# A two-layer diffusion step: the last gate blocks by token group, output weights loaded among them, projection tiles in the order of the attention, scratch tensors with long runs

## The chip, the cores and the metric

One core of a Trainium2 chip runs the whole step. The metric is the device time of one execution in microseconds (us). The engines are named as in the profile: PE (TensorE matmul), PEld (its weight load), DVE (VectorE), ACT (ScalarE), POOL (GpSimd), and SP (SyncE), which issues all the DMAs that this text speaks of from one queue, in order.

## The reference, cut to what matters

Layer 0 projects 1280 tokens (1024 latent, 256 context) into two attentions with a SiLU gate each; the gated outputs meet in one output projection. Layer 1 is a Fourier mixer with its own gate and projection.

```python
def even_lat(h, w_in, w_out, gq, gk, sink, ka_ctx, va_ctx, kb_ctx, vb_ctx, cos, sin):
    qa, ka, va, ga, qb, kb, vb, gb = even_projections(h, w_in, gq, gk)
    ...
    oa = dense_block_attention(qa, jnp.concatenate([ka, ka_ctx], axis=1),
                               jnp.concatenate([va, va_ctx], axis=1))
    ob = window_attention_with_ctx(qb, kb, vb, kb_ctx, vb_ctx, sink)
    return jnp.concatenate([oa * jax.nn.silu(ga), ob * jax.nn.silu(gb)], axis=-1) @ w_out

def odd_mix(h, w_in, w_out):
    u, gate = jnp.split(h @ w_in, 2, axis=-1)
    return (fourier_mix(u) * jax.nn.silu(gate)) @ w_out
```

## The kernel before, in words

All matmuls are float32 products made of split operands: a tensor `x` is held as `hi` and `lo`, and `mm3` adds three products. So every weight and every activation costs a copy on ACT (`hi`) and a subtraction on DVE or POOL (`lo`) before PE can use it.

The ten token tiles of 128 are worked through in units (tile, group, pair). A unit is `soft` (scores, exponentials) and, some units later, `weigh` (transposes `pt`, products `av`, a store into the DRAM scratch `od`). The tiles of mixer A come first, then those of mixer B in the order `ORD_B`. When a tile's last unit is done, `totals` sends its softmax sums through a transpose (`tt`) into the scratch `scd`.

Between units `attend` pumps a filler queue: each unit gives a credit of a few us (`FILL_B`, `FILL_C`), and queued pieces of other work are written into the program as far as the credit reaches. In order, the queue holds the remaining projections, the gate blocks `gate0` (three token groups `gi` of 512, 512 and 256 tokens, for each of eight column tiles; psum `ga`, result into scratch `gd`), the folded Fourier weights `fold_piece` (psum `wa`, result into scratch `wcd` and `wsd`), and the output projection of layer 0 by row tile. In the kernel before, the eight output weights `w_out0` are loaded and split by `out_weights` among the last eight fold pieces, into the buffers that the normalised activations (`hbufs`) held until the last gate block.

The output projection has ten steps. `proj_load` reads one row tile `r` back from `od`, `gd` and `scd` (`proj_in`), multiplies the three (`pm`), splits the product, and `proj_step` runs 48 matmuls (psum `oz`, two halves of 512 columns: `oz20` and `oz21` are the halves of row tile 2). The order of row tiles is `PAIRS`. A row tile needs certain attention tiles (`USES`: the tokens are permuted, so row tile 5 needs attention tiles 6 and 7), and `can_run` lets a load into the program only when those tiles have been finished for more than two units; from the third pair on (`EARLY`) only after the attention. In the attention the `pm` products are on POOL, after it on DVE.

A scheduler with a timeline of its own then fixes each engine's order; each engine runs its own list in order and waits by semaphores. Later, `u_load` reads the folded weights back for the Fourier mixer.

Of the kernel before, what the change touches and what calls it, by code (L numbers as in the profile page):

```python
# [28 lines left out]
ORD_B = (0, 2, 3, 4, 7, 5, 1, 6, 8, 9)  # L29
# [9 lines left out]
)  # L39
USES = ((0,), (1,), (2, 3), (2, 3), (4, 7), (6, 7), (4, 6), (5,), (8,), (9,))  # L40
# [86 lines left out]
def hybrid_step(ctx: ExitStack, tc: tile.TileContext, I, O):  # L127
# [278 lines left out]
    hbufs = []  # L406
# [27 lines left out]
    def h_slot(gi, k):  # L434
        n = GROUPS[gi][1]
        kper, slots = hT[gi]
        if k % kper == 0:
            hh = take("u", (P, kper, n * P), F32R)
            hl = take("u", (P, kper, n * P), F32R)
            slots.append((hh.a, hl.a))  # L440
            hbufs.extend([hh, hl])
        return [x[:, k % kper, :] for x in slots[k // kper]]
# [92 lines left out]
    def fold_piece(g, kb2, wu, tag="g", later=None):  # L535
# [11 lines left out]
        def put():  # L547
            rows = slice(kb2 * 256, kb2 * 256 + 256)
            sp.dma_start(wcd[g // 2, rows, g % 2, :].rearrange("(k p) f -> p k f", p=P), wo[:, :, 0:129])
            sp.dma_start(wsd[g // 2, rows, g % 2, :].rearrange("(k p) f -> p k f", p=P), wo[:, :, 128:256])  # L550
            drop(wo)
# [224 lines left out]
    def gate0(ct, gi, w):  # L776
# [10 lines left out]
        if gi < 2:  # L787
# [9 lines left out]
            sp.dma_start(gd[ct, :, t0 * P : t0 * P + 512], gs.a)  # L797
        else:
            silu(gs[:, 0:P], th[:, 0:P], acc[:, 0:P])
            silu(gs[:, P : 2 * P][:, ::-1], th[:, P : 2 * P], acc[:, P : 2 * P])  # L800
            sp.dma_start(gd[ct, :, 1024:1152], gs[:, 0:128])
            sp.dma_start(gd[ct, :, 1153:1280], gs[:, 128:255])
            sp.dma_start(gd[ct, :, 1152:1153], gs[:, 255:256])
# [174 lines left out]
    def totals(t):  # L978
# [5 lines left out]
        dve.reciprocal(tot, tot)  # L984
        tp = t_bank(f"tt{t}")
        pe.transpose(tp[0:16, 0:P], tot, ident)
        row = take("e", (16, P))
        store(scd, row, t, lambda out: act.activation(out, tp[0:16, 0:P], AF.Copy))  # L988
        drop(row)

    def store(dst, buf, t, fill):
        rev = t in (2, 3, 6, 7, 9)
        fill(buf[..., ::-1] if rev else buf.a)
        for c0, b0, n in PLACE[t]:
            sp.dma_start(dst[..., c0 : c0 + n], buf[..., b0 : b0 + n])

    def weigh(t, g, pr, bufs, p, tiles):
# [25 lines left out]
        dst = od[2 * g + pr].rearrange("(h d) n -> d h n", d=64)  # L1023
# [4 lines left out]
        def put():  # L1028
            for c0, b0, n in PLACE[t]:
                sp.dma_start(dst[..., c0 : c0 + n], os_[..., b0 : b0 + n])  # L1030
            drop(os_)
# [63 lines left out]
    for i, nm in enumerate(order):  # L1095
# [14 lines left out]
        else:  # L1110
            for c in range(2):
                for gi in range(3):
                    work.append((5.3 if gi < 2 else 2.7, lambda ct=2 * j + c, gi=gi, nm=nm: gate0(ct, gi, ws[nm])))
        nxt = loader(order[i + 1]) if 0 < i < len(order) - 1 else None
        if nxt is not None:
            fl_.add(0.0, nxt)
        after_g3 = order.index("g3") < i
        if i == order.index("g3") + 1:
            fl_.add(0.0, lambda: drop(*hbufs) or 0)
            wk_left = deque(range(8))  # L1120
            every = max(1, 4 * (len(order) - i) // 8)
            count = 0
        for n, w in enumerate(work):
            fl_.add(*w)
            if after_g3:
                count += 1
                if count % every == 0 and wk_left:
                    fl_.add(0.0, lambda k=wk_left.popleft(): wout.extend(out_weights(I["w_out0"], (k,), UV)) or 0)
        if nm[0] != "f":
            fl_.add(0.0, releaser(nm))  # L1130

# [40 lines left out]
    def proj_in(src, gate, r, resid):  # L1172
        cols = slice(r * P, r * P + P)
        if gate is not None:
            flush_held()
            ol = take(OB[0], (P, 8, P))
            sp.dma_start(ol.a, src[:, :, cols].rearrange("c p t -> p c t"))
            gl = take(OB[0], (P, 8, P))
            rl = take(OB[0], (P, 8, P))
            sp.dma_start(gl.a, gate[:, :, cols].rearrange("c p t -> p c t"))  # L1180
            sv = scd.rearrange("(c h) n -> h c n", h=2)
            for h in range(2):
                sp.dma_start(rl[64 * h : 64 * h + 64], sv[h, :, cols].unsqueeze(0).to_broadcast([64, 8, P]))
# [86 lines left out]
    half = []  # L1270
# [12 lines left out]
    def proj_step(i, j):  # L1283
# [17 lines left out]
        if r == 4:  # L1301
# [25 lines left out]
        half.append((xe, xo_))  # L1327
        if i % 2 == 0:
            return 0
        (eh, oh), (el, ol) = half  # L1330
        half.clear()
# [6 lines left out]
        if 0 in pairs[i]:  # L1338
            act.activation(op[0:1, :], oh[0:1, :], AF.Copy)
        pick("fq", E_FQ).tensor_sub(oh.a, ol.a, oh.a)  # L1340
        if 0 in pairs[i]:
            act.activation(oh[0:1, :], ol[0:1, :], AF.Copy)
        drop(ol)
        quads[pairs[i][0]] = (ep, eh, op, oh)
# [33 lines left out]
    while pend:  # L1378
        u0, pt0 = pend.pop(0)
        weigh(*u0, *pt0)  # L1380
        after(u0)
# [86 lines left out]
    def cos_src(hf):  # L1468
        return wcd[hf].rearrange("k g f -> k (g f)")

    def sin_gap(hf):
        def fn(raw, r0):
            v = raw.a.rearrange("p j (g f) -> p j g f", g=2)
            for g in range(2):
                sp.dma_start(v[:, :, g, :], wsd[hf, r0 : r0 + 2 * P, g, :].rearrange("(j p) f -> p j f", p=P))
            pool.memset(v[:, :, :, 0:1], 0.0)
        return fn

    def u_load(n):
# [14 lines left out]
        if c == 0:  # L1494
            return load_w(cos_src(hf), width=258, tags=("u", "w", "p"), each=row)
        return load_w(None, tags=BIG, gap=sin_gap(hf))
# [413 lines left out]
```

## Time and profile before

| | us |
|---|---|
| median of 3 runs | 1223.39 |
| lowest, highest | 1222.12, 1226.59 |
| profiled execution, device time | 1225.89 |
| its span, first to last instruction | 1224.1 |
| PE busy in the span | 1164.8 |
| DVE busy in the span | 841.6 |

The span is 1.8 us shorter than the device time of the same execution, and that execution is 2.5 us above the median. PE is the engine to look at: an idle microsecond of PE is a microsecond of the kernel, and one of another engine is not. The stretches that the change touches are, in the profile of before, the gate blocks (607 to 700), the folds with the output weights (700 to 747), the first three steps of the output projection beside the last attention units (747 to 795), the end of the attention (795 to 812) and the remaining steps of the projection (to about 900).

### The profile page before, as it was taken

How to read it: one execution, taken by the hardware profiler on the slowest of the kernel's cores; microseconds unless marked ns; L12 is line 12 of the kernel's file. 1: busy time of each engine (PE TensorE's matmuls, PEld its weight loads, DVE VectorE, ACT ScalarE, POOL GpSimd, SP SyncE). 2: the span in 40 equal slices, each digit the busy share in tenths (PEclk: the TensorE clock that was granted, in tenths of full speed). 3: DMA queues.
4: the chain of work that ended last, by engine and by line, in shares of the span. 5: the costliest groups of instructions: out<-in, count | busy, mean ns of one | idle time of the engine just before them, and what ended most of it. 6: DMA issues, size and time to landing. Idle time of an engine off the chain costs nothing. (4 is left out here: it accounts for less than half of the span.)

```text
span 1224.1 us, 21997 instructions
## 1 busy us (share of the span) xinstructions
PE 1164.8 (95%) x8103; PEld 1038.7 (85%) x8103; DVE 841.6 (69%) x1990; ACT 580.1 (47%) x1163; POOL 314.9 (26%) x274
## 2 busy tenths in 40 slices
PE   7879999999999999999999988989999999999997
PEld 5768889999999998999999877767877888997886
DVE  4387888877676776678878777667765963368543
ACT  4342466555565565556666676422365224332211
POOL 2254643513221231010000123120412225444001
PEclk9999999999999999999999999979999999999999
DMA  9957312323414242344233497777203435354321
GB/s 335 340 177 273 87 59 74 93 85 105 142 62 127 66 134 75 106 117 129 67 119 107 128 274 200 189 218 199 104 27 130 155 121 148 122 178 161 128 96 60
DMA packets 148688, 168.82 MB, mean 138 GB/s; under 512 B 19754, under 2 KB 107606, under 8 KB 148580
## 3 DMA queue, kind: packets, MB, share of 16 engines
q1 hardware_dynamic: 148580, 167.41, 44.1%
q8 instruction: 64, 1.05, 0.4%
q14 instruction: 44, 0.36, 0.1%
HBM read 123.19 MB, written 44.18 MB: 137 GB/s over the span
## 5 line engine op out<-in xcount | busy, mean ns | idle before, releaser
L1010 DVE TENSOR_TENSOR pt<-pt,pt 128x512 fp32r<-128x512 f32 (+1 forms) x264 | 171.3, 658 | 41.4 <-ACT pt L263 40.8
L263 ACT ACTIVATE pt<-pt 128x512 fp32r<-128x512 f32 (+1 forms) x265 | 147.4, 577 | 99.9 <-PE pt L1007 59.4
L1013 PE MATMUL av<-pt,u 128*128 128x256 f32 x1008 | 170.4, 290 | 2.2 <-DVE e L1025 1.5
L1007 PE MATMUL pt<-identr,p 128*128 128x128 f32 x1008 | 155.0, 272 | 3.0 <-ACT e L988 1.6
L1013 PEld LDWEIGHTS av<-pt,u 128*128 128x128 f32 x1008 | 140.7, 190 | 7.4 <-DVE e L1025 2.3
L251 PE MATMUL q<-w,u 128*128 128x256 f32 x864 | 133.0, 289 | 1.9 <-DVE u L427 1.6
L1007 PEld LDWEIGHTS pt<-identr,p 128*128 128x128 f32 x1008 | 118.7, 140 | 9.7 <-DVE pt L1010 2.1
L251 PE MATMUL ga<-u,w 128*128 128x512 f32 (+1 forms) x576 | 124.5, 359 | 0.0
L251 PEld LDWEIGHTS q<-w,u 128*128 128x128 f32 x864 | 116.2, 190 | 6.8 <-DVE u L427 1.9
L931 ACT ACTIVATE p<-p,nm 128x1280 f32<-128x1280 f32 (+1 forms) x80 | 95.3, 1192 | 56.1 <-DVE p L924 52.7
L251 PEld LDWEIGHTS ga<-u,w 128*128 128x128 f32 x576 | 93.8, 188 | 13.4
L269 POOL TENSOR_TENSOR w<-h,w 128x512 fp32r<-128x512 f32 x42 | 56.5, 1363 | 124.6 <-DVE w L265 87.6
L890 PE MATMUL sL<-u,q 128*128 128x512 f32 x256 | 82.2, 412 | 3.8 <-DMA q<-qd 3.7
L931 ACT ACTIVATE p<-p,NM 128x640 f32<-128x640 f32 (+2 forms) x80 | 59.1, 740 | 24.5 <-DVE p L924 24.3
L251 PE MATMUL oz<-u,u 128*128 128x512 f32 x240 | 64.3, 403 | 3.3 <-DVE h L1206 2.0
L890 PE MATMUL sC<-u,q 128*128 128x256 f32 x320 | 63.9, 299 | 1.9 <-DMA q<-qd 1.9
L269 POOL TENSOR_TENSOR u<-h,u 128x512 fp32r<-128x512 f32 x18 | 24.2, 1346 | 154.3 <-ACT u L263 139.3
L924 DVE TENSOR_SCALAR_CACHE_REDUCE p<-sL 128x512 f32<-128x512 f32 x64 | 43.8, 685 | 25.6 <-PE pt L1007 12.8
L251 PEld LDWEIGHTS oz<-u,u 128*128 128x128 f32 x240 | 45.6, 193 | 14.5 <-issue 2.4
L666 POOL TENSOR_TENSOR h<-h,rope 128x512 f32<-128x512 f32 (+1 forms) x18 | 21.6, 1203 | 139.3 <-ACT h L749 100.2
L251 PE MATMUL kv<-w,u 128*128 128x256 f32 x384 | 55.8, 288 | 0.0
L890 PEld LDWEIGHTS sC<-u,q 128*128 128x128 f32 x320 | 49.4, 190 | 5.5 <-issue 2.3
(790 smaller groups left out, 2608.4 us busy)
## 6 DMA issues: line engine op xcount, KB each, us to landing
q<-qd SPq DMA_DIRECT2D x80, 256.0 KB
p<-i_ada_w SPq DMA_DIRECT2D x21, 512.0 KB
h<-i_w_in SPq DMA_DIRECT2D x40, 256.0 KB
h<-i_w_out SPq DMA_DIRECT2D x32, 256.0 KB
pt<-i_ada_w SPq DMA_DIRECT2D x14, 512.0 KB
qd<-q SPq DMA_DIRECT2D x22, 256.0 KB
u<-g1d SPq DMA_DIRECT2D x9, 512.0 KB
w<-i_wuT SPq DMA_DIRECT2D x8, 512.0 KB
```

What stands on the lines that cost most here:

```text
L251: pe.matmul(out, a, b, start=i == 0, stop=i == n - 1)
L263: act.activation(out, in_, AF.Copy)
L269: pick("lo" + lc, lc).tensor_sub(dst_l, src, dst_h)
L666: pick("rope", XE["rope"]).tensor_mul(t1.rearrange("p t h (b c) -> p t (h b) c", b=2), y.rearrange("p t h (b c) -> p t (h b) c", b=2), cb)
L890: pe.matmul(ps, q_at(q, s, hc), keys, start=s == 0, stop=s == 1)
L924: dve.tensor_scalar(p[i][:, end[i] : end[i] + n], ps, sign, last[i], op0=ALU.mult, op1=ALU.min, accum_out=c)
L931: act.activation(p[i][:, 0 : end[i]], p[i][:, 0 : end[i]], AF.Exp, bias=last[i], scale=-1.0, accum_out=SU[:, t, hd + i, 0:1],)
L1007: pe.transpose(tp[:, jj * 256 + i * P : jj * 256 + i * P + P], p[i][:, off : off + P], ident)
L1010: dve.tensor_sub(pt[:, 1, 0:n], tp[:, 0:n], pt[:, 0, 0:n])
L1013: pe.matmul(acc, vv, pt[:, s, jj * 256 : jj * 256 + 256], start=c + jj + s == 0, stop=c + jj == nt - 1 and s == 1,)
```

## The change

Three things are done. **First**, the gate blocks of the last two weight blocks (`g2`, `g3`: four column tiles) run by token group: all four for group 0, then all four for group 1, then for group 2. After each group its `hbufs` are given back, and the output weights take their place: four weights among the blocks of group 1, four among those of group 2. The folds `f2` and `f3` follow with no output weights among them. `f2` and `f3` are also loaded only after both gate weight blocks are released. **Second**, `ORD_B` and `PAIRS` are changed: row tiles 0, 4, 2, 6 are projected first, and attention tile 6 comes sixth and no longer eighth. **Third**, `od`, `gd` and `scd` are laid out by row tile, so that a load reads runs of 4 KB where it read 512 bytes, and `wcd` and `wsd` become one `wd` with one store per fold piece. Beside this, an attention tile whose place crosses a row tile by one token is stored in two pieces (`PIECES`), a gate block of 512 tokens is stored in four runs of 512 bytes and no longer one of 2 KB, and the cosine half of the Fourier weights is read in two DMAs of 516-byte runs and no longer one of 1032.

```diff
-ORD_B = (0, 2, 3, 4, 7, 5, 1, 6, 8, 9)
+WSTEP = ((2, 1, 2), (1, 0, 1))
+ORD_B = (0, 2, 3, 4, 7, 6, 5, 1, 8, 9)
...
+PIECES = tuple(
+    tuple((r, max(c0, r * P) - r * P, b0 + max(c0, r * P) - c0, min(c0 + n, r * P + P) - max(c0, r * P))
+          for c0, b0, n in runs for r in range(c0 // P, (c0 + n - 1) // P + 1))
+    for runs in PLACE
+)
...
-PAIRS = ((3, 7), (1, 5), (2, 6), (0, 4), (8, 9))
+PAIRS = ((0, 4), (2, 6), (3, 7), (1, 5), (8, 9))
...
-ORDER = "qa0 qa1 kb0 qb0 qb1 f1 g0 g1 g2 g3 f0 f2 f3"
+ORDER = "qa0 qa1 kb0 qb0 qb1 f1 f0 g0 g1 g2 g3"
+FLATE = "f2 f3"
...
-    od = dr.tile([8, P, NT * P], F32, name="od")
-    gd = dr.tile([8, P, NT * P], F32, name="gd")
-    wcd = dr.tile([2, D, 2, 129], F32, name="wcd")
-    wsd = dr.tile([2, D, 2, P], F32, name="wsd")
+    od = dr.tile([NT, P, 8, P], F32, name="od")
+    gd = dr.tile([NT, P, 8, P], F32, name="gd")
+    wd = dr.tile([2, D, 2, 256], F32, name="wd")
...
-    scd = dr.tile([16, NT * P], F32, name="scd")
+    scd = dr.tile([NT, 2, 8, P], F32, name="scd")
...
-            sp.dma_start(gd[ct, :, t0 * P : t0 * P + 512], gs.a)
+            sp.dma_start(gd[t0 : t0 + 4, :, ct, :].rearrange("r p n -> p r n"), gs.a.rearrange("p (r n) -> p r n", r=4))
...
-            for c0, b0, n in PLACE[t]:
-                sp.dma_start(dst[..., c0 : c0 + n], os_[..., b0 : b0 + n])
+            for r, c0, b0, n in PIECES[t]:
+                dst = od[r, :, 2 * g + pr, c0 : c0 + n].rearrange("(h d) n -> d h n", d=64)
+                sp.dma_start(dst, os_[..., b0 : b0 + n])
...
+    for gi in range(3):
+        for n, (jj, c) in enumerate([(int(nm[-1]), c) for nm in order[-2:] for c in range(2)]):
+            fl_.add(*gate_work(jj, c, gi))
+            if gi > 0 and n % WSTEP[gi - 1][0] == WSTEP[gi - 1][1]:
+                wout_next(WSTEP[gi - 1][2])
+        fl_.add(0.0, lambda gi=gi: drop(*hbufs[gi]) or 0)
+    for nm in order[-2:]:
+        fl_.add(0.0, releaser(nm))
+    wout_next(len(wk_left))
+    for nm in FLATE.split():
+        fl_.add(0.0, loader(nm))
+        for k in range(4):
+            fl_.add(FC, lambda k=k, nm=nm: fold_piece(int(nm[1]), k, ws[nm]))
...
-            sp.dma_start(ol.a, src[:, :, cols].rearrange("c p t -> p c t"))
+            sp.dma_start(ol.a, src[r])
...
-                sp.dma_start(rl[64 * h : 64 * h + 64], sv[h, :, cols].unsqueeze(0).to_broadcast([64, 8, P]))
+                sp.dma_start(rl[64 * h : 64 * h + 64], scd[r, h].partition_broadcast(64))
...
-                sp.dma_start(v[:, :, g, :], wsd[hf, r0 : r0 + 2 * P, g, :].rearrange("(j p) f -> p j f", p=P))
-            pool.memset(v[:, :, :, 0:1], 0.0)
+                sp.dma_start(v[:, :, g, :], wd[hf, r0 : r0 + 2 * P, g, cols].rearrange("(j p) f -> p j f", p=P))
+            if c == 1:
+                pool.memset(v[:, :, :, 0:1], 0.0)
```

`totals` also reorders its 16 sums by a small DVE copy `byp`, ten times in all.

Line numbers of the changed program are five to fourteen above those of before for the same statement. Three places show how the order moves.

**ACT, from the first fold piece of `f2` on.** `h..<-wa20` evicts a fold piece, `u..<-h..` is the `hi` copy of an output weight that a DMA brought into `h..`, `e..<-tt7` copies the sums of tile 7. Before:

```order
L263 ACTIVATE h887_9111<-wa20_9106 128x512
L263 ACTIVATE pt915_9268<-pt7_312_9263 128x512
L1022 ACTIVATE e901_9185<-av7_30_9160 64x256
L263 ACTIVATE pt931_9360<-pt8_200_9355 128x512
L931 ACTIVATE p913_9229,SU_106<-p913_9229,NM_107 128x640
L263 ACTIVATE u920_9299<-h922_9301 128x512
L988 ACTIVATE e918_9287<-tt7_9285 16x128
L263 ACTIVATE h892_9130<-wa21_9125 128x512
L263 ACTIVATE pt952_9445<-pt8_210_9440 128x512
L263 ACTIVATE u904_9198<-h906_9200 128x512
```

Now:

```order
L269 ACTIVATE h917_9207<-wa20_9202 128x512
L936 ACTIVATE p929_9285,SU_105<-p929_9285,NM_106 128x640
L269 ACTIVATE pt931_9325<-pt7_312_9320 128x512
L1027 ACTIVATE e923_9259<-av7_30_9234 64x256
L936 ACTIVATE p929_9285,SU_105<-p929_9285,NM_106 128x640
L269 ACTIVATE pt939_9399<-pt8_200_9394 128x512
L997 ACTIVATE e934_9346<-tt7_9344 16x128
L269 ACTIVATE h918_9215<-wa21_9210 128x512
L936 ACTIVATE p937_9368,SU_105<-p937_9368,NM_106 128x640
L269 ACTIVATE pt952_9462<-pt8_210_9457 128x512
```

The two copies of output weights are gone from between the evictions; all sixteen stand earlier, among the gate blocks.

**SP, around the store of the first finished projection step (`x1d`).** `u1041` from `od` is the load of step 3 (row tile 5) before; `w1005`, `u1006` and `u1007` are the loads of step 3 (row tile 6) now. Before, with the last query load at the top:

```order
L895 DMA q1002_9875<-qd_69 64x2x512 x2
...
L1306 DMA x1d_76<-w990_9742 128x1024
L1183 DMA q1043_10188<-scd_78 64x8x128 x2
L1183 DMA u1065_10366<-scd_78 64x8x128 x2
L1195 DMA w1077_10452<-i_xp 128x1024
L1030 DMA od_72<-e1013_9963 64x2x128
L1177 DMA q1072_10439<-od_72 128x8x128
L1177 DMA u1041_10185<-od_72 128x8x128
L1195 DMA w1055_10272<-i_xp 128x1024
```

Now:

```order
L1196 DMA u1007_9926<-scd_77 64x1024 x2
...
L1191 DMA w1005_9923<-od_72 128x1024
L900 DMA q1019_10012<-qd_69 64x2x512 x2
L1194 DMA u1006_9925<-gd_73 128x1024
L1035 DMA od_72<-e992_9772 64x2x127
L1035 DMA od_72<-e992_9772 64x2x1
L1208 DMA w983_9690<-i_xp 128x1024
L1319 DMA x1d_75<-w950_9442 128x1024
```

The reads of `od` and `scd` for step 3 stood behind the second `x1d` store; they stand now, with that of `gd`, ahead of the first, around the last query load.

**PE, at the end of the attention.** `av9_31` is the last product of the last attention tile; `oz51` is step 3 before, `oz61` is step 3 now. Before:

```order
L251 MATMUL oz20_10380<-u888_9115,w1053_10268 128x512
L251 MATMUL oz20_10380<-u889_9116,w1053_10268 128x512
L1013 MATMUL av8_31_10106<-pt1030_10112,u685_7043 128x256 x4
L986 MATMUL tt9_10174<-identr_86,tot9_10168 16x128
L251 MATMUL oz51_10302<-u888_9115,q1044_10194 128x512
L251 MATMUL oz51_10302<-u889_9116,q1044_10194 128x512
L251 MATMUL oz21_10408<-u888_9115,w1053_10268 128x512
L251 MATMUL oz21_10408<-u889_9116,w1053_10268 128x512
L1013 MATMUL av9_30_10134<-pt1034_10140,u685_7043 128x256 x4
L251 MATMUL oz51_10302<-u888_9115,p1045_10195 128x512
L251 MATMUL oz51_10302<-u893_9134,q1044_10194 128x512
```

Now, first where step 3 begins, then behind the last attention product:

```order
L1012 MATMUL pt1_314_10150<-identr_85,p998_9860 128x128 x2
L257 MATMUL oz61_10332<-u817_8407,u1008_9932 128x512
L257 MATMUL oz61_10332<-u818_8408,u1008_9932 128x512
...
L1018 MATMUL av9_31_10256<-pt1046_10262,u685_7046 128x256 x4
L257 MATMUL oz70_10486<-u817_8407,pt1066_10404 128x512
L257 MATMUL oz70_10486<-u818_8408,pt1066_10404 128x512
L257 MATMUL oz71_10514<-u817_8407,pt1066_10404 128x512
L257 MATMUL oz71_10514<-u818_8408,pt1066_10404 128x512
L257 MATMUL oz11_10602<-u817_8407,u1075_10480 128x512
L257 MATMUL oz11_10602<-u818_8408,u1075_10480 128x512
L257 MATMUL oz70_10486<-u817_8407,p1067_10405 128x512
```

Step 3 was mixed with step 4 among the last products of tiles 8 and 9; it begins now some 135 rows ahead of the last product of tile 9, and what stands mixed behind that product is steps 5 and 6 (row tiles 7 and 1).

## Rows read from the trace of the kernel before

**Rows 1.** The page: busy time of each engine, share of the span, instructions.
```profile
PE 1164.8 (95%) x8103; PEld 1038.7 (85%) x8103; DVE 841.6 (69%) x1990; ACT 580.1 (47%) x1163; POOL 314.9 (26%) x274
```

**Rows 2.** Stretches: length, busy PE, PEld, DVE, ACT, POOL (xcount), clock, DMA share, GB/s.
```profile
607.00:700.00 93.00, 92.12 (x626) 84.47 (x625) 75.91 (x241) 58.89 (x139) 2.58 (x2) 1.00 0.37 109
700.00:747.00 47.00, 39.70 (x251) 34.76 (x250) 35.68 (x101) 33.75 (x78) 12.32 (x8) 1.00 0.94 262
747.00:795.00 48.00, 46.74 (x257) 39.12 (x255) 32.72 (x82) 21.98 (x53) 14.58 (x7) 1.00 0.68 183
795.00:812.00 17.00, 10.62 (x31) 7.84 (x32) 13.98 (x17) 5.74 (x10) 3.45 (x1) 0.60 0.95 276
852.00:860.00 8.00, 6.03 (x20) 4.70 (x20) 7.26 (x9) 4.01 (x6) 3.71 (x3) 0.79 0.70 213
25.00:50.00 25.00, 19.98 (x225) 16.97 (x218) 12.26 (x31) 9.25 (x16) 8.83 (x7) 0.93 0.99 333
```

**Rows 3.** Whom PE waited for, 700 to 747: us in total, times, longest.
```profile
PE wa L541 <- ACT h L263: 2.4, 2, 2.0
PE pt L1007 <- ACT e L988: 1.6, 1, 1.6
PE sC L890 <- DMA q<-qd: 1.4, 1, 1.4
PE oz L251 <- ACT h L263: 1.1, 1, 1.1
PE pt L1007 <- DVE pt L1010: 0.8, 1, 0.8
```

**Rows 4.** ScalarE in order of time: start, length, instruction, [idle before and releaser].
```profile
713.65 0.63 ACT L263 ACTIVATE u<-h 128x512 fp32r<-128x512 f32 x1 [3.23 <-DMA h<-i_w_out]
714.18 0.25 ACT L988 ACTIVATE e<-tt 16x128 f32<-16x128 f32 x1
714.34 0.57 ACT L263 ACTIVATE h<-wa 128x512 f32<-128x512 f32 x1
```

**Rows 5.** ScalarE's waits for output weights, 700 to 747.
```profile
ACT u L263 <- DMA h<-i_w_out: 11.0, 7, 3.2
```

**Rows 6.** The same, 607 to 700, and all of PE's waits there.
```profile
ACT u L263 <- DMA h<-i_w_out: 3.7, 3, 1.7
PE sC L890 <- DMA q<-qd: 0.5, 1, 0.5
PE av L1013 <- DVE pt L1010: 0.4, 1, 0.4
```

**Rows 7.** PE around the end of the attention, in order of time.
```profile
786.00 5.83 PE L251 MATMUL oz<-u,u 128*128 128x512 f32 x24
...
797.75 1.22 PE L1013 MATMUL av<-pt,u 128*128 128x256 f32 x4 [1.46 <-DVE e L1025]
...
802.91 1.22 PE L251 MATMUL oz<-u,q 128*128 128x512 f32 x2 [3.72 <-ACT q L263]
...
854.14 7.35 PE L251 MATMUL oz<-u,u 128*128 128x512 f32 x24 [1.97 <-DVE h L1206]
```

**Rows 8.** SyncE: a step's load of `od`; VectorE: the product that waited for it.
```profile
796.08 0.38 SPq L1177 DMA_DIRECT2D u<-od  x1
...
800.54 1.23 DVE L1185 TENSOR_TENSOR u<-u,u 128x1024 f32<-128x1024 f32 x1 [2.24 <-DMA u<-od]
```

**Rows 9.** Stores of `od`: times issued, shortest, median and longest issue in ns.
```profile
L1030 SPq DMA_DIRECT2D od<-e x104: 574/595/1901, 158.6 to 817.9; - x104
```

**Rows 10.** PE's waits for query tiles over the whole span.
```profile
PE sL L890 <- DMA q<-qd: 3.7, 3, 1.5
PE sC L890 <- DMA q<-qd: 1.9, 2, 1.4
```

**Rows 11.** PE's wait for fold weights, at the start of the program.
```profile
PE wa L541 <- DMA w<-i_wuT: 5.7, 1, 5.7
```

**Rows 12.** PE's only wait, 1000 to 1060.
```profile
PE u L251 <- DVE nyr L1676: 1.5, 1, 1.5
```

More of the change, by code (lines that the diff above doesn't have):

```diff
@@ L987, in totals @@
         row = take("e", (16, P))
-        store(scd, row, t, lambda out: act.activation(out, tp[0:16, 0:P], AF.Copy))
+        rev = t in (2, 3, 6, 7, 9)
+        act.activation(row[..., ::-1] if rev else row.a, tp[0:16, 0:P], AF.Copy)
+        for r, c0, b0, n in PIECES[t]:
+            sp.dma_start(scd[r, :, :, c0 : c0 + n].rearrange("h c n -> (h c) n"), row[:, b0 : b0 + n])
         drop(row)
-    def store(dst, buf, t, fill):
-        rev = t in (2, 3, 6, 7, 9)
-        fill(buf[..., ::-1] if rev else buf.a)
-        for c0, b0, n in PLACE[t]:
-            sp.dma_start(dst[..., c0 : c0 + n], buf[..., b0 : b0 + n])
     def weigh(t, g, pr, bufs, p, tiles):
@@ L1093, in releaser, with gate_work, wout_next @@
         return fn
-    for i, nm in enumerate(order):
+    def gate_work(j, c, gi):
+        return (5.3 if gi < 2 else 2.7, lambda: gate0(2 * j + c, gi, ws[f"g{j}"]))
+    wk_left = deque(range(8))
+    def wout_next(n):
+        for _ in range(n):
+            fl_.add(0.0, lambda k=wk_left.popleft(): wout.extend(out_weights(I["w_out0"], (k,), UV)) or 0)
+    for i, nm in enumerate(order[:-1]):
         j = int(nm[-1])
@@ L1109, in hybrid_step @@
                 work.append((FC, lambda k=k, nm=nm, j=j: fold_piece(j, k, ws[nm])))
[L1110 to L1123, printed above, removed]
-            fl_.add(*w)
[L1125 to L1129, printed above, removed]
-            fl_.add(0.0, releaser(nm))
+        elif i < len(order) - 2:
+            work += [gate_work(j, c, gi) for c in range(2) for gi in range(3)]
+        if i > 0:
+            fl_.add(0.0, loader(order[i + 1]))
+        for w in work:
+            fl_.add(*w)
+        if i < len(order) - 2 and nm[0] != "f":
+            fl_.add(0.0, releaser(nm))
+    for gi in range(3):
[11 more added lines that the diff above has]
+            fl_.add(FC, lambda k=k, nm=nm: fold_piece(int(nm[1]), k, ws[nm]))
     lastA = {g: (NT - 1, g, 1) for g in range(2)}
@@ L1269, in hybrid_step @@
     kept = []
-    half = []
+    half = {}
     ins = {}
@@ L1326, in proj_step @@
             return 0
-        half.append((xe, xo_))
+        half[pairs[i][0]] = xe, xo_
         if i % 2 == 0:
             return 0
-        (eh, oh), (el, ol) = half
-        half.clear()
+        z = 0 in half
+        (eh, oh), (el, ol) = half.pop(2 if z else 3), half.pop(0 if z else 1)
         ep = take(OB[0], (P, D))
@@ L1380, in hybrid_step @@
         weigh(*u0, *pt0)
+        flush_held()
         after(u0)
@@ L1494, in u_load @@
         if c == 0:
-            return load_w(cos_src(hf), width=258, tags=("u", "w", "p"), each=row)
-        return load_w(None, tags=BIG, gap=sin_gap(hf))
+            return load_w(None, width=258, tags=("u", "w", "p"), gap=u_gap(c, hf), each=row)
+        return load_w(None, tags=BIG, gap=u_gap(c, hf))
     def table(src, n):
```

36 lines of the change are left out of this document (17 added, 19 removed).

## The prediction

> **What bounds the kernel now.** I read the page first: PE is busy 1164.8 of the span's 1224.1 us, 95% [rows 1], so only PE's idle and slow time can be won, some 59 us over the whole span. Next I asked for the stretches that the change touches [rows 2]; idle PE time is length less busy time. Among the gate blocks PE is idle 0.9 us of 93, in the folds 7.3 of 47, beside the first projection steps 1.3 of 48, at the end of the attention 6.4 of 17, and 2.0 in the eight from 852. The same rows give the granted clock: 0.60 at the end of the attention and 0.79 from 852, so part of the time went at 1.2 GHz, the lower of the two levels, after PE had stood idle. Taking the mean clock for the busy time, an estimate, that cost 10.62 x 0.40 = 4.2 us and 6.03 x 0.21 = 1.3 us. So the change can win at most 7.3 at the folds, 10.6 at the end of the attention and 3.3 later: 21 us in all. Everything below asks how much of these three pots it reaches, and what it costs in stretches that are now full.
>
> Then the waits. In the folds PE waited 2.4 us for ACT's eviction of a fold piece, 1.6 for ACT's copy of the softmax sums, 1.1 for a last eviction, 0.8 for a probability tile and 1.4 for a query load [rows 3]. ACT's own list says why [rows 4]: it stood 3.23 us for an output weight still on its way, and behind that copy, in order, came the sums and the eviction that PE wanted. ACT lost 11.0 us in seven such waits [rows 5], with the DMA engines 94% busy [rows 2]. At the end of the attention the longest wait is 3.72 us for ACT's `hi` of step 3 [rows 7]. Followed back: SP issued the step's read of `od` at 796.08, DVE waited for it until 800.54 [rows 8], and PE started at 802.91, 6.8 us after the issue.
>
> **The change part by part.**
>
> *Folds without output weights.* The ACT rows in the section on the change show that no weight copy is left between the evictions. That removes the cause of 2.4 + 1.6 + 1.1 us; the 0.8 I count with them, since ACT's backlog makes a probability tile late too. The 1.4 for the query load I halve: thirteen loads of 256 KB leave a stretch that moved 262 GB/s x 47 us = 12.3 MB, but reads for two more projection steps come in. What is late next there is ACT's `hi` of row tile 0, which now stands among the evictions and waits for POOL's products; I give 0.7 for it. Sum: -5.9 - 0.7 + 0.7 = **-5.9** (bounds -7.3 and -3).
>
> *The weights among the gate blocks.* Sixteen copies stand there, where three waits already lay. Those three cost ACT 3.7 us, and PE lost 0.9 in the whole stretch, of which 0.4 was of the kind that a late ACT makes [rows 6]: 0.13 per wait. At the folds a wait cost PE 5.9 / 7 = 0.84. The gate blocks give PE more to do between attention pieces than the short fold pieces, and the DMA share is 0.37 [rows 2]; thirteen loads add 3.4 MB to the 10 MB of the stretch, which makes it about 0.50. So I stay near the lower price: 13 x 0.13 = **+1.7** (bounds 0 and 13 x 0.84 = 11). The copies and subtractions themselves hide under PE: ACT has 34 us free of 93, DVE 17, POOL 90.
>
> *Fold weights later.* `f2` and `f3` can be loaded only when the gate weights are released. Their 2 MB at 262 GB/s are 8 us; two gate blocks and some attention lie between the release and the first fold piece. The one time that PE is seen to wait for such a load, with nothing else to do, it took 5.7 us [rows 11]. Bounds 0 and 5.7; I take **+0.5**, as the cover is there.
>
> *Step 3 earlier.* Its loads now stand ahead of the first `x1d` store and used to stand behind the second. One step lies between the two stores: 2 x 5.83 = 11.7 us of matmuls [rows 7], more than the 6.8 us from issue to first matmul. So the 3.72 us wait should go. Its products move too: the load is now in the program before the attention ends, so POOL makes the two 1.23 us products of [rows 8], at its own speed, and POOL is busy only 3.45 of 17 us there. Of the other 2.7 us of idle I take half, 1.3, and of the 4.2 us of slow clock 3.0, since the clock fell after PE had idled. **-8.0** (bounds 0 and -10.6). What is late next: steps 5 and 6, whose first matmuls stand right behind the last product of tile 9.
>
> *From 852.* PE waits for DVE to free a psum bank [rows 7], DVE being busy 7.26 of 8. The new order changes what DVE has queued, and nothing shows which way; **-0.7** of a possible 3.3.
>
> *Short pieces.* Three more attention tiles are stored in two pieces, 24 more stores than the 104 of before, and three more for the sums. At 595 ns each [rows 9] SP spends 14 us more over 660. What waits behind them on SP is query loads, and PE waits for those five times in the whole span, 5.6 us in all [rows 10]. Growing with the number of stores that is 1.3; a bound below is 0; I take **+0.5**. The gate stores in four runs and the ten small copies on DVE have nothing behind them that PE wants.
>
> *Fourier weights in two reads.* PE's only wait there is 1.5 us, for DVE and not for a load [rows 12], so **0** (bounds 0 and +1.5). SP issues eight more loads ahead of use.
>
> Sum: -5.9 + 1.7 + 0.5 - 8.0 - 0.7 + 0.5 = -11.9. The profiled execution took 1225.9 us, so 1214.0; it was 2.5 above the median, so **1211.5** on the scale of the runs.
>
> *Are longer runs worth anything?* Per unit of DMA share the folds moved 262 / 0.94 = 279 GB/s, and the start, which reads inputs and weights in runs of 1 KB and more, 333 / 0.99 = 336 [rows 2]. A step reads 1.5 MB in 512-byte runs: 5.6 us at the one rate, 4.7 at the other, so nearly 1 us per step. The Trainium skill, "DMA: Bandwidth & Descriptors", section Specifications, says that 512 bytes is the smallest transfer at line rate and that less makes the engine read, modify and write. By that rule the reads gain nothing; the rows of other stretches disagree so far, though they mix kinds of traffic.
>
> **The rivals.**
>
> *DVE binds the end of the attention.* DVE is busy 13.98 of the 17 us [rows 2]. If its list there stays as full, PE can regain 3.0 and no more, and not 8.0: -6.9, 1216.5. For it: two products of 128x1024 are only 2.5 us of what DVE does. Against it: its waits for `od` [rows 8] are inside the idle part, and the work comes earlier.
>
> *The weight waits travel.* If a wait in the gate stretch costs what one costs at the folds, the second term is 11 and not 1.7: -2.6, 1220.8. For it: the same in-order ACT. Against it: [rows 6].
>
> *Longer runs bring nothing.* The order alone hides step 3, so this takes only 1.0 us off that term: 1212.5. This is what the page's rule would make of it.
>
> *Everything comes back.* All three pots and no new cost: 1225.9 - 21.2 - 2.5, about 1202.
>
> *Slower: the short pieces hold up the query loads.* 128 runs of 4 bytes are a whole DMA on the one queue that also brings queries. If each of the 24 extra ones ended in a query wait of the mean seen, 5.6 / 5 = 1.1 us, that is 27 us and not 0.5: 1238. It decides from 12.4 / 24 = 0.52 us of PE time per piece. Against it: 24 such pairs are in the kernel before, and even if they caused all five waits, that is 0.23 each. The rule above on transfers under 512 bytes speaks for slow pieces; no row here times one.
>
> That the change does nothing is out: the three pieces of the order show the moves.
>
> **How the numbers follow.** A measurement of this kernel can tell about 0.5%, 6 us, from no change: 1217.3 to 1229.5 is the middle class. My forecast of 1211.5, with its own range 1207 to 1216, gets 0.45; DVE as the bound 0.17, half of it faster; travelling waits 0.10, nearly all in the middle; longer runs worth nothing 0.10 and everything back 0.12, both faster; short pieces 0.06, slower. With some blur at the edges: 0.76 faster, 0.17 within, 0.07 slower. The range 1203 to 1220 leaves out half of "everything back", more than half of the travelling waits, and the short pieces: 0.17.
>
> **What would show it.** In the profile after: no wait of ACT for `i_w_out` in the folds and PE idle there under 2 us; such waits among the gate blocks, with PE idle there still under 3; step 3's first matmul with no wait, and the granted clock above 0.8 through the end of the attention; four pairs of products on POOL. I am wrong if PE idles more than 4 us among the gate blocks, if the first fold piece waits for its weights, if a wait of 3 us or more stands before steps 5 or 6, or if PE's waits for query loads double.

## The result

The changed kernel takes 1214.24 us (median of 7 runs, 1212.19 to 1222.20) beside 1224.73 us for the kernel before (7 runs, on the same chip). The ratio is 0.9923, with a 95% interval of 0.9895 to 0.9952. So 10.5 us are gone where 11.9 were forecast. The profiled execution took 1214.73 us.

The page after, as [rows 1]:
```profile
PE 1162.7 (96%) x8103; PEld 1038.2 (86%) x8103; DVE 842.6 (69%) x1997; ACT 580.5 (48%) x1163; POOL 321.9 (27%) x277
```

To see where the time went I cut both executions at the same four events: the first and the last matmul of a gate block, the first matmul of a projection step (`oz`), the last attention product (`av`), and the first matmul of the next stage (`g1E`). These are stretches of the kernel before; columns as in [rows 2]:
```profile
467.80:700.70 232.90, 231.92 (x1548) 211.61 (x1547) 174.60 (x539) 141.20 (x313) 13.73 (x13) 1.00 0.35 101
700.70:745.70 45.00, 37.70 (x240) 32.98 (x238) 34.38 (x98) 32.27 (x75) 12.17 (x8) 1.00 0.95 264
745.70:814.60 68.90, 61.27 (x305) 50.24 (x306) 49.48 (x104) 29.80 (x65) 18.03 (x8) 0.90 0.74 204
814.60:891.70 77.10, 74.09 (x320) 59.56 (x318) 51.58 (x70) 20.60 (x31) 18.62 (x12) 0.98 0.49 145
```

And the same stretches of the changed kernel, with a fifth row for the 17 us of [rows 2] in which the clock had been 0.60:
```profile
466.30:701.40 235.10, 232.65 (x1546) 211.34 (x1545) 180.38 (x552) 147.07 (x326) 21.36 (x18) 1.00 0.40 111
701.40:747.80 46.40, 39.82 (x246) 35.57 (x244) 34.26 (x98) 28.60 (x66) 9.93 (x5) 0.96 0.90 242
747.80:814.70 66.90, 65.42 (x341) 54.90 (x342) 43.71 (x108) 28.35 (x66) 19.15 (x10) 1.00 0.61 184
814.70:881.40 66.70, 64.00 (x282) 50.65 (x281) 50.87 (x63) 21.87 (x35) 19.06 (x12) 1.00 0.53 162
795.00:812.00 17.00, 17.00 (x86) 14.17 (x85) 12.99 (x17) 4.33 (x8) 2.21 (x1) 1.00 0.66 202
```

The gate blocks cost 2.2 us (232.9 to 235.1). The folds, to the first `oz`, got 1.4 us longer, with the same 64 fold matmuls in them; PE idles 6.6 us there where it idled 7.3. From there to `g1E` it went from 146.0 to 133.6 us, 12.4 less: PE idles 1.5 us where it idled 7.6 (66.90 - 65.42 beside 68.90 - 61.27), the clock is at its upper level all through, and about one projection step more is done before the attention ends (217 `oz` matmuls in the trace, beside 175; a step has 48). The remaining 2.4 of the 11.2 us by which the span is shorter lie ahead of the first gate block (1.5) and behind `g1E` (0.9).

The folds are where the forecast failed, and the view of PE's waits from 701 to 748 says by what, beside [rows 3]:
```profile
PE sC L895 <- DMA q<-qd: 5.6, 3, 3.4
PE oz L257 <- ACT h L269: 0.5, 1, 0.5
PE pt L1012 <- DVE pt L1015: 0.2, 1, 0.2
```
The waits for ACT of [rows 3] are down to 0.5 us, as foreseen, and 5.6 us for query tiles stand in their place. The longest, followed back on SP (start, issue time, instruction) and then on PE:
```profile
702.54 0.52 SPq L1292 DMA_DIRECT2D u<-gtd  x1
703.10 0.45 SPq L1191 DMA_DIRECT2D u<-od  x1
703.65 0.47 SPq L1196 DMA_DIRECT2D u<-scd  x1
704.56 0.58 SPq L900 DMA_DIRECT2D q<-qd  x1
...
708.29 0.57 SPq L900 DMA_DIRECT2D q<-qd  x1
```
```profile
715.58 0.47 PE L895 MATMUL sC<-u,q 128*128 128x256 f32 x2 [3.41 <-DMA q<-qd]
...
718.54 2.69 PE L547 MATMUL wa<-h,w 128*128 128x256 f32 x8
...
724.86 1.99 PE L547 MATMUL wa<-h,w 128*128 128x256 f32 x8
```
Three of the reads of projection step 0 stand ahead of the query on SP, four stores stand between the query's halves, and PE gets the second half 7.3 us after its issue. The fold piece behind the wait took 2.69 us and the one after it 1.99 us: the clock had dropped (0.68 in the 3.5 us from 715.5).

Step 3 starts at 798.17 with no wait, where [rows 7] had 3.72 us. The longest wait for DVE behind the attention, 1.97 us at 854.14 in [rows 7], is 1.31 us now, at another place in the steps:
```profile
798.17 3.04 PE L257 MATMUL oz<-u,u 128*128 128x512 f32 x12
...
835.17 0.74 PE L257 MATMUL oz<-u,u 128*128 128x512 f32 x2 [1.31 <-DVE h L1219]
```

### The profile page after: what moved, and what is told of

It reads as the page before. It is cut to its first block, busy times and chain, and to the rows that moved or that the text cites. A ratio compares the mean times of both kernels' runs of the same rounds, so it can differ in the third digit from the quotient of the medians.

```text
span 1212.9 us, 22074 instructions
## 1 busy us (share of the span) xinstructions
PE 1162.7 (96%) x8103; PEld 1038.2 (86%) x8103; DVE 842.6 (69%) x1997; ACT 580.5 (48%) x1163; POOL 321.9 (27%) x277
## 2 busy tenths in 40 slices
DMA packets 129328, 168.81 MB, mean 139 GB/s; under 512 B 26298, under 2 KB 86454, under 8 KB 129220
## 5 line engine op out<-in xcount | busy, mean ns | idle before, releaser
L275 POOL TENSOR_TENSOR u<-h,u 128x512 fp32r<-128x512 f32 x24 | 35.2, 1473 | 141.5 <-ACT u L269 111.2
L257 PE MATMUL oz<-u,u 128*128 128x512 f32 x224 | 61.7, 398 | 1.8 <-DVE h L1219 1.3
L1027 ACT ACTIVATE e<-av 64x256 f32<-64x256 f32 x80 | 30.5, 382 | 46.1 <-PE av L1018 40.0
```

The costliest lines, as they stand in the source:

```text
L257: pe.matmul(out, a, b, start=i == 0, stop=i == n - 1)
L275: pick("lo" + lc, lc).tensor_sub(dst_l, src, dst_h)
L1027: act.activation(lo_sb.a, a3[64:128], AF.Copy)
```

## The experiments

### Which part gives the time

The change has three parts that can be built one by one: the order (A), the gate blocks by token group with the weights among them and two fold weights last (B), and the scratch layout (C). With the kernel before and the changed one, six more kernels give all eight combinations. The first three are the kernel before with one part each; their diffs are those parts of the change:
```
e1_order
-ORD_B = (0, 2, 3, 4, 7, 5, 1, 6, 8, 9)
+ORD_B = (0, 2, 3, 4, 7, 6, 5, 1, 8, 9)
-PAIRS = ((3, 7), (1, 5), (2, 6), (0, 4), (8, 9))
+PAIRS = ((0, 4), (2, 6), (3, 7), (1, 5), (8, 9))
...
e2_gates
-ORDER = "qa0 qa1 kb0 qb0 qb1 f1 g0 g1 g2 g3 f0 f2 f3"
+ORDER = "qa0 qa1 kb0 qb0 qb1 f1 f0 g0 g1 g2 g3"
+FLATE = "f2 f3"
...
e3_runs
-    od = dr.tile([8, P, NT * P], F32, name="od")
+    od = dr.tile([NT, P, 8, P], F32, name="od")
...
```

> The kernel before with the order alone (order of the attention tiles, pairs of projection steps, and what the pairing needs); the old gate blocks and the old scratch layout. Theory: the matching order alone removes the late step 3 and the slow clock behind it, so the end of the attention and the stretch behind it give 10 to 13 us back as in the whole change, and the folds stay as they were, with the weight waits of ACT; total -9 to -13 us. Rival: the gain at the end of the attention needs the long runs too, since a step's reads would otherwise still be late; then a wait of over 2 us stays before a step and the total is -3 to -6 us.

> The kernel before with the gate blocks by token group, the output weights among them and two fold weights last; old order, old scratch layout. Theory: the DMA engines are full in the folds whatever is taken out, since the reads of the projection steps move up into the room; ACT's weight waits go, query waits of 2 us or more come in their place, and the total is -2 to +2 us. Rival: the query waits in the folds come from the short pieces of the new layout, which are not in this kernel; then the folds gain their 6 us, the gates cost 2, and the total is -3 to -5 us with query waits in the folds under 1.5 us.

> The kernel before with the scratch layout alone (long runs for the attention output, the gates, the sums and the folded weights; three more tiles stored in two pieces). Theory: the reads get some 1 us shorter a step, most of it beside other work, and the short pieces cost about as much: -2 to +1 us. Rival 1: the long runs carry a good part of the gain by themselves, step 3's wait of 3.7 us shrinks by 1 us or more, -3 to -6 us. Rival 2: the short pieces hold up the queries, PE's query waits rise from 5.6 us to 9 us or more and the total is +3 us or more.

The other three join two parts: `e4_order_gates` is A and B, `e9_order_runs` A and C, `e10_gates_runs` B and C, without further edits.

> The whole change without the new scratch layout (order and gate blocks as after, layout as before). Theory: the late queries in the folds come from full DMA queues and not from the short pieces, so a wait of 2 us or more for a query stays in the folds and the time is within 3 us of the changed kernel (ratio 0.990 to 0.995). Rival: the short pieces are the cause; the query waits in the folds go under 1.5 us and the time is 4 us or more below the changed kernel (ratio under 0.989). Second rival: the long runs are worth 5 us or more by making reads cheaper; ratio over 0.996.

> The kernel before with the order and the new scratch layout, but the old gate blocks (one block's three token groups after another, the output weights and all buffers of the normalized input released behind the last). Theory: the order needs the gate blocks by token group, since the order alone gave nothing, order with grouping gave all, and the place of the weights made no difference; without the grouping a later step's read is late again, and the ratio is 0.996 to 1.001. Rival: either of the other two parts is enough for the order, the layout too; ratio 0.990 to 0.994.

> The changed kernel without the new order (old order of the attention tiles and old pairs of steps; gate blocks and layout as changed). Theory: without the order step 3 is late at the end of the attention whatever the rest does: a wait of 3 us or more there with a fallen clock behind it, ratio 0.996 to 1.001. Rival: grouping and layout together bring the reads early enough; ratio 0.990 to 0.994 and no wait over 2 us at the end of the attention.

What was measured (ratio to the kernel before, 95% interval), the time in the profile from the last gate matmul to the first `g1E`, and PE's longest wait for a projection step or for the last products around the end of the attention:

| parts | ratio | interval | last gate to `g1E`, us | longest wait there, us |
|---|---|---|---|---|
| none | 1 | | 191.0 | 3.72, step 3 |
| A (e1) | 1.0018 | 1.0002 to 1.0034 | 191.0 | 4.72, step 5 |
| B (e2) | 1.0019 | 1.0001 to 1.0038 | 189.9 | 4.9, step 3 |
| C (e3) | 0.9971 | 0.9950 to 0.9992 | 188.5 | 4.7, step 3 |
| B, C (e10) | 0.9997 | 0.9978 to 1.0015 | 186.3 | 2.61, step 3 |
| A, C (e9) | 0.9925 | 0.9904 to 0.9946 | 182.6 | 4.29, last product; 2.36, step 5 |
| A, B (e4) | 0.9911 | 0.9883 to 0.9939 | 180.1 | 0.6 |
| A, B, C | 0.9923 | 0.9895 to 0.9952 | 180.0 | 0.5 |

Three things follow. **The order is necessary:** each of the four kernels with the old order waits 2.6 to 4.9 us for step 3, and none gains more than 0.3%. **The order alone is not enough:** my theory for `e1_order` fell, and its rival had the wait right but not the time. Step 3 is in time, but step 5 is not, whose first matmuls stand right behind the last product; the wait is for ACT's `hi` of it:
```profile
831.85 2.07 PE L251 MATMUL oz<-u,pt 128*128 128x512 f32 x4 [4.72 <-ACT pt L263]
```
and the mean clock is 0.93 over the 70 us behind the attention. **Either other part is enough beside the order,** so the gains do not add: A and B alone are each 0.2% slower, together 0.9% faster, and C on top of both is worth nothing that can be measured. For `e9_order_runs` the rival was right.

The other forecasts: `e2_gates` had the waits right (4.4 us for queries in the folds, none of ACT for weights) and the time just outside its range, at +2.3 us by the ratio. `e3_runs` gained 3.6 us, more than its theory gave it; its first rival had that time, but step 3's wait grew to 4.7 us where the rival had it shrink. For `e4_order_gates` the theory was right (a query wait of 3.0 us). For `e10_gates_runs` the theory had the time and the place, with 2.6 us where it had said 3 or more.

Why step 5 is late in one kernel and not in the other can be followed on SP. The step's last read, of `gd`, stands behind step 6's read of `od`, and in `e1_order` that one waited for the landing of an `od` store. A row of SP's waits, 805 to 831, and then SP in order of time:
```profile
SPq L1177 <- DMA od<-e: 3.8, 1, 3.8
```
```profile
817.58 0.38 SPq L1177 DMA_DIRECT2D p<-od  x1
...
822.48 0.52 SPq L1180 DMA_DIRECT2D pt<-gd  x1
```
The last product ended at 827.1, 4.6 us after that read went out, and ACT had the `hi` ready at 831.8. In the changed kernel no such wait stands there; the row of SP, and ACT's `hi`:
```profile
800.90 0.31 SPq L1191 DMA_DIRECT2D p<-od  x1
...
805.72 0.37 SPq L1194 DMA_DIRECT2D pt<-gd  x1
```
```profile
813.38 1.04 ACT L269 ACTIVATE pt<-p 128x1024 fp32r<-128x1024 f32 x1
```
Here the read goes out 9.0 us before the last product ends at 814.7, and the `hi` is ready at 814.4, just in time; in `e4_order_gates` it is 8.7 us and again just in time. In `e9_order_runs` it is 10.3 us and the `hi` is 2.4 us late all the same: the read is there 6.8 us after its issue, beside 4.5 in the changed kernel, and then DVE and ACT put other work between. DVE's first product with it, in `e9_order_runs` and in the changed kernel:
```profile
813.42 1.23 DVE L1185 TENSOR_TENSOR pt<-pt,p 128x1024 f32<-128x1024 f32 x1 [0.96 <-DMA pt<-gd]
```
```profile
810.19 1.22 DVE L1197 TENSOR_TENSOR pt<-pt,p 128x1024 f32<-128x1024 f32 x1 [0.20 <-DMA pt<-gd]
```

Step 5 is the smaller part of the difference. With the order, all four kernels have 586 to 589 matmuls in the trace between the last gate block and the last attention product, and 281 or 282 from there to `g1E`, so these two stretches can be compared. The first takes 120.6 us with the order alone, 115.4 with A and C, 114.9 with A and B and 113.3 in the changed kernel; the second takes 70.4, 67.2, 65.2 and 66.7. So 3 to 5 us of the gain lie behind the last product, where step 5 is waited for, and 5 to 7 us ahead of it. There the order alone leaves PE waiting mostly for DVE (706.5 to 827.1 in `e1_order`):
```profile
PE av L1013 <- DVE e L1025: 4.3, 4, 1.9
PE sC L890 <- DVE p L968: 3.2, 2, 1.6
```
Why the grouping or the layout shortens the way to the last product, and gives step 5 its lead, stays open. The grouping changes what buffers are free when, and no run isolates a buffer; the layout takes time off the DMA engines in just this stretch, as the part on longer runs below shows.

### The weights' place

The output weights are the part that my fold term spoke of. Here they alone go back:
```
e5_weights_folds (the changed kernel with)
-            if gi > 0 and n % WSTEP[gi - 1][0] == WSTEP[gi - 1][1]:
-                wout_next(WSTEP[gi - 1][2])
...
-    wout_next(len(wk_left))
...
             fl_.add(FC, lambda k=k, nm=nm: fold_piece(int(nm[1]), k, ws[nm]))
+            wout_next(1)
```

> The changed kernel with the output weights back among the last eight fold pieces, one after each, as before; the gate blocks stay grouped by token group. Theory: the place of the weights is what the matching order needs. ACT waits 8 us or more for them among the folds again, and behind it PE waits for DVE and ACT after the folds, as with the order alone; the time goes back to that of the kernel before (ratio 0.997 to 1.003). The gate stretch loses its 2 us cost. Rival: the gain hangs on the grouping of the gate blocks, which frees buffers sooner, so that the steps' reads start earlier; then the ratio stays at 0.990 to 0.995 with the weights in either place.

Measured 0.9922 (0.9899 to 0.9946): the rival was right. ACT's waits from 700 to 770 are back, longer than in [rows 5], and the gate stretch has its 2.2 us back (a row of ACT's waits, and the stretch from first to last gate matmul):
```profile
ACT u L269 <- DMA h<-i_w_out: 16.2, 9, 3.8
```
```profile
469.80:702.50 232.70, 231.31 (x1546) 211.51 (x1545) 175.30 (x544) 139.59 (x311) 12.14 (x11) 1.00 0.37 96
```
So it is the weights, not the grouping, that cost 2.2 us among the gates, and their move by itself is worth nothing: the folds are 46.3 us long with ACT waiting for weights (9.9 of the 16.2 us fall in them) and 46.4 without. From the first gate to `g1E` this profile is 3.1 us shorter than the changed kernel's (412.0 beside 415.1) and 3.5 us longer ahead of it, where neither has weights or folds to move; over all runs the ratios are the same.

The second part of the fold term is the fold weights' place. In this kernel they come ahead of the gate blocks:
```
e8_folds_first (the changed kernel with)
-ORDER = "qa0 qa1 kb0 qb0 qb1 f1 f0 g0 g1 g2 g3"
-FLATE = "f2 f3"
+ORDER = "qa0 qa1 kb0 qb0 qb1 f1 f2 f3 g0 g1 g2 g3"
+FLATE = ""
```

> The changed kernel with the last two fold weights and their pieces ahead of the gate blocks, so that 2 MB of reads and the folded weights' stores leave the stretch before the first projection step. Theory: the query waits there come from full DMA engines; with less to move they go under 2 us in all, and the time falls by 2 to 5 us against the changed kernel (ratio 0.988 to 0.991). Rival: gate blocks and output weights come later by the time of the fold pieces, ACT's waits for weights now lie where the steps begin, and the time is 2 to 6 us above the changed kernel (ratio 0.994 to 0.998).

Measured 1.0035 (1.0018 to 1.0052). The rival had the place, with 8.4 us of ACT's waits for weights from 700 to 760, and too small a size. No query wait of over 0.84 us is left between 690 and 905, but PE waits for the attention's own chain and for step 0 instead, which I put down to the fold pieces missing as work beside the last attention tiles; no run shows that apart:
```profile
748.46 1.22 PE L257 MATMUL oz<-u,w 128*128 128x512 f32 x2 [2.23 <-ACT w L269]
...
824.90 1.23 PE L1018 MATMUL av<-pt,u 128*128 128x256 f32 x4 [3.71 <-DVE e L1029]
```

### What makes the queries late

One suspect is the short pieces:
```
e7_whole (the changed kernel with)
-    for runs in PLACE
+    for runs in [((r * P, 0, P),) for r in (0, 1, 3, 2, 6, 7, 5, 4, 8, 9)]
...
-            sp.dma_start(gd[9, :, ct, 1:P], gs[:, 128:255])
-            sp.dma_start(gd[9, :, ct, 0:1], gs[:, 255:256])
+            sp.dma_start(gd[9, :, ct, :], gs[:, 128:256])
```

> The changed kernel with every attention tile, its sums and the last gate tile stored in one piece, to the row tile that holds most of it: left out is the shift by one column of the reversed tiles. 48 one-column stores of the attention output, six of the sums and eight of the gates are gone. Theory: the pieces cost SP's time and DMA time that lies beside other work: 0 to -2 us against the changed kernel (ratio 0.991 to 0.993), query waits in the folds still over 3 us in all. Rival: they are what makes the queries late; the waits in the folds go under 1.5 us and the time falls by 4 us or more (ratio under 0.989).

Measured 0.9916 (0.9890 to 0.9941), the theory. PE's waits from 703 to 752:
```profile
PE sC L894 <- DMA q<-qd: 6.2, 2, 3.4
PE wa L547 <- ACT h L269: 0.3, 1, 0.3
```
The pieces are not the cause, and all 48 of the attention output together cost less than can be measured. The queries are late exactly where the weights have left the folds: PE's waits at `sC` come to 6.0, 5.6, 6.5, 6.2 and 5.6 us in `e2_gates`, `e4_order_gates`, the changed kernel, `e7_whole` and `e10_gates_runs`, and to 0.4 to 2.8 us in the six others that keep a query's two places (before, e1, e3, e5, e8 and e9, with the weights in the folds or the folds out of the way).

The other suspect is that a query waits for one of its two places. This gives it a third:
```
e6_q_third (the changed kernel with)
-        q = take("q", (P, 2, 512))
+        q = take(("q", "w") if g > 1 else "q", (P, 2, 512))
```

> The changed kernel with a third place for a query tile in the second half of the attention (a query may also take a buffer of the weights' zone), so that its load stands ahead of step 0's reads in SP's row and not behind them. Theory: queries are late in the folds because a load can be issued only when one of two places comes free, and by then the first step's 2 MB stand ahead of it; the 3.4 us wait goes under 1 us and the time falls by 2 to 5 us against the changed kernel (ratio 0.988 to 0.991). Rival: the DMA engines are simply full; what is not waited for at the query is waited for at the first projection steps (2 us or more there), ratio 0.991 to 0.995.

Measured 0.9862 (0.9836 to 0.9887), 1208.79 us: the fastest kernel of the study, some 7 us faster than the changed one by the two ratios. But the step that I gave for it holds for one tile only. SP's row and then PE's:
```profile
703.02 1.22 SPq L900 DMA_DIRECT2D w<-qd  x2
704.66 0.33 SPq L1292 DMA_DIRECT2D u<-gtd  x1
...
711.96 1.33 SPq L1208 DMA_DIRECT2D w<-i_xp  x1
713.39 0.60 SPq L900 DMA_DIRECT2D q<-qd  x1
```
```profile
721.93 0.80 PE L895 MATMUL sC<-u,q 128*128 128x256 f32 x2 [4.18 <-DMA q<-qd]
```
The query at 703.02 goes out ahead of step 0's reads and PE does not wait for it. The next one stands behind all of them and is waited for 4.18 us. A later one, in the new place, is waited for too:
```profile
767.15 0.47 PE L895 MATMUL sC<-u,w 128*128 128x256 f32 x2 [1.68 <-DMA w<-qd]
```
So PE's waits for queries come to 10.5 us over the whole span where the changed kernel has 11.1: hardly any of the 7 us is won in the waits for queries themselves. The rival's wait at the first steps is not there either. The folds are 41.2 us long beside 46.4 (PE idle 4.2 us beside 6.6), and behind the last product PE is busy for all of 61.95 us, where the changed kernel took 66.7 with 2.7 idle. That the place causes this is shown by the edit, which is one line; by what chain it clears the waits behind the attention is not settled.

Two more kernels ask whether the third place is worth this anywhere: `e11_before_q` has that line in the kernel before, `e12_q_weights_folds` has it in `e5_weights_folds`.

> The kernel before with only the third place for a query tile in the second half of the attention. Theory: there the queries are late for 1.4 us in the folds, and what binds is ACT behind its weight copies and step 3's read, which the third place doesn't touch: -2 to +1 us (ratio 0.998 to 1.001). Rival: a third place is worth its 5 us in any kernel, since it lets the softmax run ahead of PE; ratio 0.994 to 0.997.

> The changed kernel with the third place for a query tile and with the output weights back among the last fold pieces. Theory: the weights cost 2 us among the gate blocks, which come back, and in the folds ACT's waits for them lie behind nothing that PE wants, as they did when only their place was put back: ratio 0.983 to 0.986, the fastest. Rival: with the query waits gone from the folds, ACT's weight waits are what ends last there; the 2 us are lost again or more, ratio 0.986 to 0.990.

Measured 1.0033 (1.0017 to 1.0050) and 0.9918 (0.9900 to 0.9936). In the first, both theories missed: it is slower, with 5.21 us for step 3 where [rows 7] had 3.72:
```profile
808.34 1.22 PE L251 MATMUL oz<-u,q 128*128 128x512 f32 x2 [5.21 <-ACT q L263]
```
In the second the rival was right in kind: PE has no wait for a query at `sC` at all, and in the folds it waits for ACT, which waits 14.0 us for weights there:
```profile
741.41 3.65 PE L547 MATMUL wa<-h,w 128*128 128x256 f32 x8 [3.74 <-ACT h L269]
```
So the third place pays only where the weights have left the folds, and the weights' move pays only with the third place: 0.9922 with neither (`e5_weights_folds`), 0.9923 and 0.9918 with one of them, 0.9862 with both.

## Why the prediction was right, and where not

The median came out 2.7 us from the forecast, inside its narrow range, but two of its terms were wrong in opposite directions. The folds came out 6.8 us worse than forecast (+1.4 for -5.9 and +0.5), the end of the attention with what follows 3.7 us better, and 2.4 us were won ahead of the gate blocks and behind `g1E`, where the forecast had nothing but part of the +0.5 for short pieces. That these nearly cancel is luck.

- **Folds without output weights, -5.9: this step failed.** "That removes the cause of 2.4 + 1.6 + 1.1 us" was true of the cause; the time did not follow. The stretch got 1.4 us longer. I halved the query wait on the ground that the loads had left; in fact the reads of the next steps moved up into the room: the weights' 3.1 MB are gone, the reads issued for the steps rose from 4.0 to 6.5 MB, and 11.42 MB moved in the 47 us from 701, beside 12.31 in those from 700. The query wait went from 1.4 to 5.6 us, and PE idles 6.6 us in the folds where I had asked for under 2. The sign that I had named, PE's query waits doubling, came: [rows 10] add up to 5.6 us, the same rows after to 11.1.
```profile
PE sC L895 <- DMA q<-qd: 6.5, 4, 3.4
PE sL L895 <- DMA q<-qd: 4.6, 4, 1.7
```
- **Weights among the gate blocks, +1.7: right,** 2.2 in the profile, 1.5 of it idle time of PE. With the weights there, the stretch from first to last gate matmul is 234.7 to 235.7 us in five kernels and 237.2 in `e7_whole`; with the weights in the folds it is 232.7 to 233.1 in six and 234.4 in `e12_q_weights_folds` (`e8_folds_first` has fewer matmuls in that stretch and is left out). The rival with 11 us is out.
- **Fold weights later, +0.5:** PE never waited for one; 0.
- **Step 3 earlier, -8.0, and from 852, -0.7: the mechanism was right, the size too small.** Beside the 8.7 us forecast stand 12.4. The 3.72 us wait, the rest of the idle time and all of the slow clock went from these 17 us (17.00 busy at clock 1.00, where [rows 2] had 10.62 at 0.60); I had kept back half of the small idle and 1.2 of the clock's 4.2 us. The longest wait for DVE behind the attention fell by 0.66. POOL makes four pairs of products where it made three, as forecast.
- **The working treated the terms as a sum, and they are not.** I wrote that the order alone hides step 3; it does, and then waits for step 5, one of the two that I had named as late next, and for DVE ahead of the last product, which I had not. The -8.0 belongs to the order with one of the other two parts.
- **Short pieces, +0.5, and Fourier weights in two reads, 0:** nothing measurable (the 27 stores at 595 ns make 16 us of SP's time and not 14; nothing hangs on it), and PE has no wait at all from 1000 to 1050, where it had that of [rows 12]. The slower rival is out: removing 48 one-column stores changed nothing that can be measured (0.9916 beside 0.9923).
- **Are longer runs worth anything?** I took nearly 1 us a step, by rates of mixed stretches, and put no term for it in the sum. As time of the DMA engines it was right. Queue 1 from the last gate block to `g1E` (packets, MB, share of the 16 engines), with the order alone over 191.0 us and with order and layout over 182.6 us:
```profile
q1 hardware_dynamic: 46803, 36.97, 72.0%
```
```profile
q1 hardware_dynamic: 18381, 36.94, 67.4%
```
That is 137.5 us of the engines and 123.1 for the same bytes. In the three other pairs with and without the layout the difference is 7 to 11 us, so over ten steps 0.7 to 1.4 us a step, with some saving on the folded weights' stores in it. The whole program hides this, since the layout also adds packets elsewhere (the gate stores in runs of 512 bytes, more short pieces). In the pages' DMA part, before, after and with whole pieces:
```profile
DMA packets 148688, 168.82 MB, mean 138 GB/s; under 512 B 19754, under 2 KB 107606, under 8 KB 148580
q1 hardware_dynamic: 148580, 167.41, 44.1%
```
```profile
DMA packets 129328, 168.81 MB, mean 139 GB/s; under 512 B 26298, under 2 KB 86454, under 8 KB 129220
q1 hardware_dynamic: 129220, 167.40, 44.3%
```
```profile
DMA packets 121072, 168.80 MB, mean 139 GB/s; under 512 B 10778, under 2 KB 78198, under 8 KB 120964
q1 hardware_dynamic: 120964, 167.39, 44.3%
```
Share times span, the packets took 540, 537 and 537 us of the 16 engines. Over all kernels it was 540 to 559 us in five with the old layout and 537 to 549 in the nine with the new one. In the kernel's time the rival that longer runs bring nothing held for the changed kernel: the layout is worth nothing on top of the other two parts, 0.3% by itself and 0.9% beside the order alone. Its reason did not hold. The Trainium skill, "DMA: Bandwidth & Descriptors", section Specifications, has 512 bytes as enough for line rate, and a read-modify-write below that. The traces hold each packet's time and agree with neither: in the changed kernel the median is 27 ns for 512 bytes and 159 ns for 4 KB, so that eight short packets take 216 ns for the bytes of one long one, and it is 28 ns for 508 bytes and 9 ns for 4 bytes, so that no price of going below 512 bytes shows.
- **DVE as the bound at the end of the attention:** out; DVE is busy 12.99 of the 17 us and PE all of them.

## What to carry to other kernels

A wait that is removed from a full stretch is worth only the distance to the next one: ask of the row behind it what will be late then, and look at whatever the scheduler moves into the freed room before counting the gain. Parts of a change that shorten the same chain are tested in combinations, since each alone may show nothing or a loss while together they give the whole. A further place for a fetched tile was worth some 7 us in one kernel, nothing in a second and a loss in a third, so it is worth trying again after each wait that is removed.

## What was not expected of the hardware

A packet's time on a DMA engine showed no step at 512 bytes: the medians in the changed kernel are 9 ns for 4 bytes, 28 for 508, 27 for 512, 46 for 1 KB, 84 for 2 KB and 159 for 4 KB. So one-column stores are cheap for the engines (well over half of the packets under 512 bytes were gone with whole pieces, 26,298 and 10,778, at the same 537 us), and by these medians 512-byte runs cost a third more than 4 KB runs of the same bytes. And 3.4 us of idle time on PE were enough for the next matmuls to run slower, with the mean clock of that stretch at 0.96.
